# Two-layer encoder on one core: queries and keys of the first head group by seven half-sized products before the attention, kept in DRAM, with changes of order beside it

## The chip, the core and the metric

The program runs on one core of a Trainium2 chip. A core has engines that run side by side, each with its own instruction queue worked off in order: TensorE (PE, matrix products, with PEld for the loading of weights), VectorE (DVE), ScalarE (ACT), GpSimd (POOL) and SyncE (SP). SP only starts transfers here; POOL computes a little and starts the transfers that add to what is already in their destination. They meet at semaphores. The metric is the device time of one execution in microseconds (us), as a median of several executions. Before the change it is 1441.67 us (three executions, 1441.1 to 1444.09).

## What is computed

The input is x, 512 tokens by 1024 features in float32. Two layers follow each other, each with a token mixer and an MLP, and in front of each of these an RMS norm with a gain. The first mixer is the one that the change is about:

```python
def dilated_mixer(h, w_qkv, q_gain, k_gain, w_o):
    qkv = (h @ w_qkv).reshape(B, S, 3, N_GROUPS, A_HEADS, A_HEAD_DIM)   # 512 x 1024 by 1024 x 9216
    for g, (window, dil) in enumerate(DIL_CONFIGS):                     # 3 groups
        q = rope(rms_norm(qkv[:, :, 0, g], q_gain[g]), S)
        k = rope(rms_norm(qkv[:, :, 1, g], k_gain[g]), S)
        v = qkv[:, :, 2, g]
        o, lse = dilated_group(q, k, v, window, dil)                    # softmax over a dilated band
    wts = jax.nn.softmax(jnp.stack(lses, 0), axis=0)
    o = sum over g of wts[g] * o[g]
    return o.reshape(B, S, A_WIDTH) @ w_o
```

There are eight heads of 128 features in each of three groups. Per group the queries of all heads are 1024 columns of the product, the keys 1024 and the values 1024. The second mixer (multi-head latent attention) and the two MLPs (1024 to 4096, squared ReLU, back to 1024) are untouched but for one step of order.

## The kernel before

**Precision.** Products are made in three passes: each operand is split into a rounded high part and the rest (`whi`, `wlo` of a weight, made by one ACT copy and one DVE subtraction), and high by high, high by low and low by high are added up in a PSUM bank. A pass over 128 rows of the contraction and 512 columns is one matmul instruction.

**Stages.** (1) `v_phase` (line 306) norms x, turns it into `hT` and computes the values of the three groups. (2) The attention (lines 542 to 749) goes through four pairs of heads, `b` = 0 to 3. (3) The output projection, (4) the first MLP, (5) the latent attention, (6) its projection and the second MLP.

**Half-sized products in `v_phase`.** The values of a group are one product of 512 tokens by 1024 by 768 columns (the seventh and eighth head are done elsewhere). Tokens, contraction and columns are each halved, and the four quarter results are put together from seven products of quarters where plain blocks would need eight (Winograd's form of Strassen's scheme). The sums of the left operand are prepared once (`Ssp`, from `dif` and `h32`). The weight quarters `b21`, `b11`, `b12`, `b22` are loaded by SP; their sums `bT` are made by DVE (`sum1`, line 446) and by two transfers of POOL that add a further quarter into `bT` (`add_block`, line 329). `piece` (line 450) does products 5, 3, 6, 7 and 4 and puts the results together in `vo`; finished parts go to DRAM (`vall`). A product is 24 matmuls of 384 columns, and each weight quarter lies in one of five places of the ring `wq`. `dif` and `rot` (rotary tables and gains of the first group, which `tables(0, ...)` multiplies) have places of their own.

**Attention.** For each pair of heads and each group `project_in` (line 709) computes queries and keys together, 512 columns, by `qk_proj` (line 297): four token tiles of 24 matmuls, in one of four PSUM banks `acc` each; the weights come as `raw` (three places) and are split by lines 156 and 157. `qk_evac` (line 265) then works off a tile `acc`: four ACT squares with sums, three DVE products with the rotary tables (lines 276 and 279), the power -0.5 on POOL (`rstd_of`, line 131), a DVE sum and a DVE scaling (284 and 285), four PE transposes, and an ACT copy into `qkT`, which has two places. `scores` does the banded softmax; `finish` merges the groups and multiplies with the values. The loop of lines 722 to 734 projects one group ahead: the scores of group g, then the projection of g + 1, and after the third group the projection of the next pair's first group, ahead of `finish`.

**What sets the order.** The kernel is traced in this program order, and the framework's scheduler (`schedule_with_timeline_sim=True`) then orders each engine's queue by program order and by its own simulated times. So an engine's queue need not be in program order: matmuls of a later projection can stand between those of `scores`. Once built, each queue is fixed.

**End of the first MLP.** `wino` (line 759) is the MLP's own form of seven products. `fetch(..., add=True)` (line 779) has POOL start transfers that add a weight quarter in place. The tables `cgB` and `sgB` of the latent attention (lines 963 to 968) are nine POOL instructions further down in the program.

## Time and profile before

| quantity | value |
|---|---|
| median of three executions | 1441.67 us (1441.1 to 1444.09) |
| the profiled execution's own time | 1438.6 us |
| its span, from the first to the last instruction | 1436.8 us |
| mean granted TensorE clock | 0.997 |
| HBM read, written | 180.85 MB, 7.86 MB |
| `v_phase` | about 0 to 128 us of the span |
| attention, to its last merged heads | about 128 to 500 us |
| output projection and first MLP | about 500 to 894 us |
| latent attention | about 894 to 1080 us |
| its projection and second MLP | about 1080 to 1437 us |

The profile is of one execution; its own time is 3.1 us under the median. A row of the windows view gives, for a stretch of time, its length, then for PE, PEld, DVE, ACT and POOL the busy time with the count of instructions in brackets, then the granted TensorE clock, the busy share of the 16 DMA engines, and GB/s. A matmul's duration overlaps with that of the next one, so a row that shows PE fully busy can hide gaps shorter than that overlap; what a matmul costs in a dense row is the stretch divided by the count. A row of the chain of waits or of the timeline gives start, length, engine, what it is and how many instructions were merged; in square brackets stands how long the engine sat idle before it, and what ended that.

### The profile page before, as it was taken

To read this page: it belongs to the slowest core of one execution; us is meant where nothing else is said; L and a number is where in the kernel's file an instruction comes from. 1 tells how busy PE (TensorE), PEld (TensorE's weight loads), DVE (VectorE), ACT (ScalarE), POOL (GpSimd) and SP (SyncE) were. 2 spreads that over 40 slices of the span, in tenths; PEclk is the share of its full clock that TensorE was granted. 3 is DMA by queue.
4 is the path that set the end of the run, shared out by engine and by line. 5 is a ranking of instruction groups with operands and counts; after the bars stand their busy time and mean duration, and the time that the engine had idled before them with its cause. 6 is when DMAs were issued, how large, how long until landed. Compare 5 with 4: busy or idle time off the path is not lost.

```text
span 1436.8 us, 19234 instructions
## 1 busy us (share of the span) xinstructions
PE 1398.5 (97%) x7044; PEld 1184.7 (82%) x7044; DVE 928.6 (65%) x1485; ACT 746.6 (52%) x1626; POOL 213.0 (15%) x209
## 2 busy tenths in 40 slices
PE   6999999999999999999999998999999999999998
PEld 6899888988888988888888887776768888888886
DVE  6765878676886754465564758688755266475647
ACT  5553656464564623553545455787633453544543
POOL 0120121122111101020110231332201011020201
PEclk9999999999999999999999999999999999999999
DMA  9767322332322345667493934311014759394835
GB/s 310 189 167 207 117 88 72 107 93 83 117 75 68 114 134 191 175 137 216 116 235 101 213 93 84 96 31 30 30 45 149 203 112 239 90 230 135 190 90 117
DMA packets 127614, 189.97 MB, mean 132 GB/s; under 512 B 8608, under 2 KB 66208, under 8 KB 127520
## 3 DMA queue, kind: packets, MB, share of 16 engines
q1 hardware_dynamic: 106848, 150.47, 32.8%
q0 software_dynamic: 20672, 38.28, 16.2%
q8 instruction: 55, 0.90, 0.3%
q14 instruction: 39, 0.32, 0.1%
HBM read 180.85 MB, written 7.86 MB: 131 GB/s over the span
## 4 chain that ended last, share of the span: by engine, by line
PE 87%; DMA 4%; ACT 3%; DVE 3%; issue 1%; POOL 1%; SPq 0%; ACTq 0%; DVEq 0%; POOLq 0%
PE acc L184 51%; PE sc L850 11%; PE tp L850 8%; PE tp L123 4%; PE sc L422 2%; PE acc L1134 1%; PE acc L1110 1%; PE sc L1028 1%; DMA b<-in_a_w_qkv_dram 1%; PE sco L699 1%; PE sc L585 1%; PE sco L695 1%; PE tp L422 1%; DMA bT<-in_a_w_qkv_dram 1%; DMA raw<-in_a_w_qkv_dram 1%
## 5 line engine op out<-in xcount | busy, mean ns | idle before, releaser
L184 PE MATMUL acc<-whi,hT 128*128 128x512 f32 (+2 forms) x1216 | 383.2, 389 | 2.8 <-ACT hT L737 1.3
L184 PE MATMUL acc<-hT_f,whi 128*128 128x512 f32 (+1 forms) x1152 | 318.6, 366 | 1.7 <-DVE resid L913 1.2
L157 DVE TENSOR_TENSOR wlo<-raw,whi 128x1024 fp32r<-128x1024 f32 (+3 forms) x146 | 172.2, 1187 | 172.5 <-ACT whi L156 171.9
L184 PEld LDWEIGHTS acc<-whi,hT 128*128 128x128 f32 x1216 | 225.8, 188 | 44.0 <-ACT hT L737 1.9
L156 ACT ACTIVATE whi<-raw 128x1024 fp32r<-128x1024 f32 (+3 forms) x146 | 149.5, 1031 | 177.2 <-PE acc L184 83.8
L184 PEld LDWEIGHTS acc<-hT_f,whi 128*128 128x128 f32 x1152 | 208.2, 189 | 37.3 <-DVE resid L913 1.6
L184 PE MATMUL acc<-wlo,hT 128*128 128x512 f32 (+2 forms) x608 | 236.0, 389 | 0.7 <-DVE wlo L157 0.7
L794 DVE TENSOR_TENSOR wlo<-wqs,whi 128x1024 fp32r<-128x1024 f32 x112 | 137.4, 1226 | 112.9 <-ACT whi L793 112.7
L184 PE MATMUL acc<-hT_f,wlo 128*128 128x512 f32 (+1 forms) x576 | 204.9, 366 | 0.0
L793 ACT ACTIVATE whi<-wqs 128x1024 fp32r<-128x1024 f32 x112 | 118.8, 1060 | 165.6 <-PE acc L184 66.2
L850 PE MATMUL sc<-whi,asp 128*128 128x512 f32 x512 | 165.6, 391 | 4.9 <-ACT whi L793 4.7
L779 POOL DMA_DIRECT2D wqs<-in_ffn_w_dram x64 | 77.6, 1341 | 513.3 <-DVE wlo L794 331.2
L184 PEld LDWEIGHTS acc<-wlo,hT 128*128 128x128 f32 x608 | 114.4, 188 | 19.4 <-DVE wlo L157 1.0
L184 PEld LDWEIGHTS acc<-hT_f,wlo 128*128 128x128 f32 x576 | 108.5, 189 | 17.5
L850 PEld LDWEIGHTS sc<-whi,asp 128*128 128x128 f32 x512 | 96.2, 188 | 25.9 <-ACT whi L793 5.2
L850 PE MATMUL tp<-whi,asp 128*128 128x512 f32 x352 | 112.8, 392 | 0.9 <-DVE resid L824 0.9
L131 POOL TENSOR_TENSOR qrs<-rs_v,nhalf 128x4 f32<-128x4 f32 x48 | 61.2, 1279 | 305.7 <-DVE rs_v L128 265.6
L850 PE MATMUL sc<-wlo,asp 128*128 128x512 f32 x256 | 99.6, 389 | 0.0
L136 ACT ACTIVATE junk<-acc 128x128 f32<-128x128 f32 x192 | 52.8, 275 | 53.9 <-PE acc L184 48.0
L850 PEld LDWEIGHTS tp<-whi,asp 128*128 128x128 f32 x352 | 66.7, 190 | 15.3 <-DVE resid L824 1.3
L850 PE MATMUL tp<-wlo,asp 128*128 128x512 f32 x176 | 68.7, 392 | 0.0
L824 DVE TENSOR_TENSOR resid<-resid,sc 128x512 f32<-128x512 f32 x64 | 43.1, 681 | 26.3 <-PE sc L850 26.3
(229 smaller groups left out, 2171.5 us busy)
## 6 DMA issues: line engine op xcount, KB each, us to landing
wqs<-in_ffn_w_dram SPq DMA_DIRECT2D x80, 512.0 KB, 5.1
raw<-in_ffn_w_dram SPq DMA_DIRECT2D x64, 512.0 KB, 4.5
wqs<-in_ffn_w_dram POOLq DMA_DIRECT2D x64, 512.0 KB, 7.4
raw<-in_a_w_qkv_dram SPq DMA_DIRECT2D x96, 256.0 KB, 3.2
b<-in_a_w_qkv_dram SPq DMA_DIRECT2D x24, 384.0 KB, 6.2
vall<-vo SPq DMA_DIRECT2D x24, 192.0 KB, 3.6
bT<-in_a_w_qkv_dram POOLq DMA_DIRECT2D x12, 384.0 KB, 6.1
raw<-in_a_w_o_dram SPq DMA_DIRECT2D x8, 512.0 KB, 3.8
```

The costliest lines, as they stand in the source:

```text
L123: PE.transpose(o, i, ident)
L131: G.tensor_tensor(out, v[:, :n], nhalf[:, :n], op=ALU.pow)
L136: A.activation(junk, x, AF.Square, scale=1.0 / math.sqrt(dim), accum_out=out)
L156: A.activation(hi[:, :nk, :n], raw[:, :nk, :n], AF.Copy)
L157: V.tensor_tensor(lo[:, :nk, :n], raw[:, :nk, :n], hi[:, :nk, :n].bitcast(F32), op=ALU.subtract)
L184: PE.matmul(accs[o][:, oc], lhsT=lt, rhs=rt, start=(kt == 0 and p_i == 0 and hv == 0), stop=(kt == total - 1 and p_i == 2), skip_group_che ...
L422: PE.matmul(banks[t][:, :VH], lhsT=lt, rhs=rt[:, j], start=(first and k == 0 and i_ == 0), stop=(k == 3 and i_ == 2), skip_group_check=True)
L779: nc.gpsimd.dma_start(t, src, accum_op=ALU.add)
L793: A.activation(hi, x, AF.Copy)
L794: V.tensor_tensor(lo, x, hi.bitcast(F32), op=ALU.subtract)
L824: V.tensor_tensor(sl, sl, banks[t], op=op)
L850: PE.matmul(bk[t], lhsT=lt, rhs=rt[:, j], start=(first and k == 0 and i_ == 0), stop=(k == 3 and i_ == 2), skip_group_check=True)
```

## The change

Queries and keys of the first group (`g` = 0) leave `project_in`. They are computed in `v_phase`, between the values of the first group and those of the second, as two more units of seven products (a new class `Unit` stands for a weight matrix with its quarters): unit f takes query columns 512 f to 512 f + 511 as its left half and the key columns of the same range as its right half, so that a quarter is 512 columns wide and a product is 24 matmuls of 512 columns. The results go to two DRAM buffers `qk0`. In the attention `project_in(b, 0)` loads a tile of 128 tokens by 2 x 256 columns from there, for each of four token tiles, and gives it to `qk_evac` in the place of the PSUM bank; the rest of `qk_evac` is as before.

Beside it: the loop projects two groups ahead (the second group of a pair is projected before the scores of its first); `load_x(0)` comes ahead of the load of the gain; `rot` and the first group's gains are loaded, and its `tables` made, after the first unit, in the ring `xn`; `dif` lies in the ring `wq`; the ring `wq` and `vo` are 512 columns wide; and the nine POOL instructions of `cgB` and `sgB` are queued behind the last adding transfer of the first MLP (`tc.issue_after`, which orders them on POOL's queue alone).

```diff
+    qk0 = [ad.tile([S, D], F32, name=f"qk0{t}") for t in range(2)]
...
-        rot = vp.tile([P, D], F32, name="rot")
-        dif = vp.tile([P, 2, 2, 4, P], F32, name="dif")
...
+        class Unit:
+            def __init__(self, width, cols, out):
+                self.w, self.cols, self.out, self.parts = width, cols, out, {}
...
+            def tile(self, name, tag="wq", bufs=5):
+                return vp.tile([P, 4, 512], F32, tag=tag, name=nm(name), bufs=bufs)[:, :, :self.w]
...
+            def fetch(self):
+                self.b21, self.b11 = self.block(1, 0, "b21"), self.block(0, 0, "b11")
+                self.fetch_more()
+                self.bT = self.tile("bT")
...
+        vals = [Unit(VH, lambda n, g=g: w6[:, :, 2, g, VH * n:VH * n + VH],
+                     lambda i, n, g=g: by_tiles(vall[g], i, slice(VH * n, VH * n + VH))) for g in range(NG)]
+        qks = [Unit(512, lambda n, f=f: w6[:, :, n, 0, 512 * f:512 * f + 512],
+                    lambda i, n, f=f: by_tiles(qk0[n], i, slice(512 * f, 512 * f + 512))) for f in range(2)]
...
+        load_x(0)
         gain_b = gain_table(norm_mix[0:1, :].rearrange("o d -> (o d)"), D, "g_mix0")
-        load_x(0)
...
+        dif = vp.tile([P, 4, 512], F32, tag="wq", name="dif", bufs=5)
+        dif = dif.rearrange("p (n i) (k t) -> p n i k t", n=2, k=4)
         raw6.append(load_raw(*units6[3], 384))
-        nc.sync.dma_start(rot[:, 0:C_M1 - C_KEEP], consts[:, C_KEEP:C_M1])
-        g0 = rot[:, 768:1024].rearrange("p (t d) -> p t d", t=2)
-        load_gains(0, g0)
...
-        piece(0, ba)
+        piece(v0, ba)
+        rot = vp.tile([P, D], F32, tag="xn", name="rot", bufs=2)
+        nc.sync.dma_start(rot[:, 0:C_M1 - C_KEEP], consts[:, C_KEEP:C_M1])
+        g0 = rot[:, 768:1024].rearrange("p (t d) -> p t d", t=2)
+        load_gains(0, g0)
         tables(0, g0, rot[:, 0:256], rot[:, 256:768])
-        for g in range(1, NG):
...
+        for un in qks + vals[1:]:
+            un.fetch()
             bd, ba = new_banks("d"), new_banks("a")
+            both(un, 2, un.b21, bd, True)
+            put(un, 0, 0, "set", bd, False)
+            both(un, 1, un.b11, ba, True)
+            put(un, 0, 0, "add", ba, True)
+            for u in range(2):
+                sum1(un, u)
+            piece(un, ba)
...
             qkT = aw.tile([P, 4, S], F32, tag="qkT", name=nm("qkT"))
-            qk_proj(b, g, qkT, homes, junk)
+            if g:
+                qk_proj(b, g, qkT, homes, junk)
+                return qkT
+            for r in range(NT):
+                x = aw.tile([P, 2, 256], F32, tag="qk0", name=nm("qk0"), bufs=3)
+                for t in range(2):
+                    nc.sync.dma_start(x[:, t], qk0[t].rearrange("(m r) d -> m r d", r=NT)[:, r, 256 * b:256 * b + 256])
+                qk_evac(0, qkT, r, x.rearrange("p t c -> p (t c)"), homes, junk)()
             return qkT
...
-        qkT = project_in(0, 0)
+        qkT, nxt = project_in(0, 0), project_in(0, 1)
         for b in range(HA // 2):
...
-            for g in range(NG):
-                scores(b, g, qkT, Pt, stats)
-                if g + 1 < NG:
-                    qkT = project_in(b, g + 1)
+            scores(b, 0, qkT, Pt, stats)
+            qkT = nxt
+            scores(b, 1, qkT, Pt, stats)
+            qkT = project_in(b, 2)
+            scores(b, 2, qkT, Pt, stats)
             if b + 1 < HA // 2:
-                qkT = project_in(b + 1, 0)
+                qkT, nxt = project_in(b + 1, 0), project_in(b + 1, 1)
                 finish(b, Pt, stats, vs)
...
-                    nc.gpsimd.dma_start(t, src, accum_op=ALU.add)
+                    marks["sum"] = nc.gpsimd.dma_start(t, src, accum_op=ALU.add).ins
...
+            with tc.issue_after(marks["sum"]):
+                for t in range(2):
+                    for hf in range(2):
+                        gb = gr[:, t, hf * 32:hf * 32 + 32].unsqueeze(1).broadcast_to([P, NT, 32])
+                        G.tensor_tensor(cgB[:, :, t, hf * 32:hf * 32 + 32], cosB, gb, op=ALU.mult)
+                        G.tensor_tensor(sgB[:, :, t, hf * 32:hf * 32 + 32], sinB, gb, op=ALU.mult)
+                G.tensor_scalar(sgB[:, :, :, 32:64], sgB[:, :, :, 32:64], -1.0, None, op0=ALU.mult)
```

More of the change, by code (lines that the diff above doesn't have):

```diff
@@ L421, in product, with both @@
                 for i_, (lt, rt) in enumerate(((ah, hi), (ah, lo), (al, hi))):
-                    PE.matmul(banks[t][:, :VH], lhsT=lt, rhs=rt[:, j], start=(first and k == 0 and i_ == 0),
+                    PE.matmul(banks[t][:, :un.w], lhsT=lt, rhs=rt[:, j], start=(first and k == 0 and i_ == 0),
                               stop=(k == 3 and i_ == 2), skip_group_check=True)
-        def both(p, w, banks, first):
+        def both(un, p, w, banks, first):
             for u, t in ((0, 0), (0, 1), (1, 0), (1, 1)):
-                product(p, w, banks, first, u, t)
+                product(un, p, w, banks, first, u, t)
         def new_banks(chain):
@@ L509, in v_phase @@
             s2(i)
-        split(5, bT[0], 0)
-        split(5, bT[0], 1)
+        split(v0, 5, v0.bT, 0)
+        split(v0, 5, v0.bT, 1)
         for i in range(2):
```

140 lines of the change are left out of this document (59 added, 81 removed).

## The prediction

> **What bounds the kernel now.** I read the page's busy shares first, then the chain that ended last, then the windows view over the stages, then who PE waited for.
>
> ```profile
> PE 1398.5 (97%) x7044; PEld 1184.7 (82%) x7044; DVE 928.6 (65%) x1485; ACT 746.6 (52%) x1626; POOL 213.0 (15%) x209
> ...
> PE 87%; DMA 4%; ACT 3%; DVE 3%; issue 1%; POOL 1%; SPq 0%; ACTq 0%; DVEq 0%; POOLq 0%
> ```
> ```profile
> 63.00:95.00 32.00, 31.34 (x178) 30.36 (x177) 20.61 (x27) 16.71 (x24) 4.81 (x4) 1.00 0.76 199
> 95.00:128.00 33.00, 33.00 (x190) 32.78 (x190) 20.14 (x25) 16.09 (x24) 4.81 (x4) 1.00 0.57 133
> ...
> 130.00:480.00 350.00, 349.78 (x1922) 300.33 (x1921) 258.25 (x514) 191.69 (x670) 59.88 (x47) 1.00 0.32 99
> ```
> ```profile
> PE acc L184 <- DVE rs_v L128: 0.2, 1, 0.2
> ```
> ```profile
> 103.06 4.16 PE sc L422 x24
> ...
> 128.95 20.91 PE acc L184 x92
> ```
>
> The first fence says that 87% of the chain is matmuls. The second shows two units of `v_phase` and, below, the attention: there PE is busy for 349.78 of 350 us, DVE for 258.25 (74%), ACT for 191.69 (55%). The third is all that PE waited for in the attention: 0.2 us. So the attention is PE's, to the last matmul, and what is taken from PE there is won until DVE stands in the way. The fourth gives prices: a matmul of 512 columns costs 20.91 / 92 = 0.2273 us in a dense row, one of 384 columns 4.16 / 24 = 0.173 us.
>
> **The products.** Removed from the attention: 4 pairs x 4 token tiles x 24 = 384 matmuls, 384 x 0.2273 = 87.3 us of PE. Added to `v_phase`: 2 units x 7 products x 24 = 336, or 76.4 us. Net **-10.9 us**, if both places stay as dense as they are. The rest of the sum is whether they do.
>
> **The POOL tables at the end of the first MLP.** The second MLP runs the same last seven products without tables beside them, so it shows what their move is worth.
>
> ```profile
> 847.62 0.39 PE L850 MATMUL sc<-whi,asp 128*128 128x512 f32 x1
> ...
> 868.83 1.22 PE L850 MATMUL sc<-whi,asp 128*128 128x512 f32 x2 [4.73 <-ACT whi L793]
> ...
> 889.90 1.04 PE L123 MATMUL tp<-ck,xn 128*128 128x128 f32 x8
> ```
> ```profile
> 850.85 0.54 POOL L966 TENSOR_TENSOR cgB<-ck,gr 128x128 f32<-128x128 f32 x1 [26.59 <-DMA gr<-in_b_q_gain_dram]
> ...
> 859.36 1.71 POOL L968 TENSOR_SCALAR sgB<-sgB 128x256 f32<-128x256 f32 x1
> 861.03 2.50 POOL L779 DMA_DIRECT2D wqs<-in_ffn_w_dram  x2
> ...
> 884.49 0.57 POOL L131 TENSOR_TENSOR nrs<-rs_v,nhalf 128x1 f32<-128x1 f32 x1 [9.86 <-DVE rs_v L128]
> ```
> ```profile
> 868.70:872.10 3.40, 3.27 (x8) 2.63 (x9) 3.15 (x4) 1.35 (x3) 1.20 (x1) 0.50 0.19 34
> ```
> ```profile
> 881.61 8.45 PE sc L850 x36
> ...
> 1421.89 11.18 PE sc L850 x48
> ```
> ```profile
> 1393.25 0.39 PE L850 MATMUL sc<-whi,asp 128*128 128x512 f32 x1
> ```
> ```profile
> 1415.36 1.20 POOL L779 DMA_DIRECT2D wqs<-in_ffn_w_dram  x1 [1.67 <-DVE wlo L794]
> ```
> ```profile
> L219 DVE SCALAR_TENSOR_TENSOR xn<-resid,nrs,g_mix x4: 1276/1280/1284, 885.3 to 900.9; 128x1024 f32<-128x1024 f32 x4
> ```
>
> The tables hold POOL from 850.85 to 861.07; the adding transfers start at 861.03 behind them, and PE stands still for 4.73 us, after which its clock is at half for 3.4 us. From the first matmul of the seven products to their last block it is 881.61 - 847.62 = 33.99 us here and 1421.89 - 1393.25 = 28.64 us in the second MLP: **-5.3 us** when the tables go. They don't vanish: the last add ends at 1415.36 + 1.20 - 545.63 (the distance of the two starts) = 870.9, the tables then need their 10.2 us, to 881.1, and the power of the next norm, at 884.49 - 5.3 = 879.2, would wait 1.9 us. The scaling that needs it ends at 885.3 + 1.3 = 886.6, and PE asks for it at 889.90: 3.3 us of cover, so I cost this at nothing. Were the cover gone, 1.9 us would come back. Range of the term -5.4 to -3.4.
>
> **The start.**
>
> ```profile
> 0.74 0.39 SPq L232 DMA_DIRECT2D g_mix<-in_norm_mix_dram  x1
> ...
> 1.18 0.90 SPq L335 DMA_DIRECT2D xts<-in_x_dram  x2
> ...
> 7.18 1.06 ACT L136 ACTIVATE xn<-xts 128x1024 f32<-128x1024 f32 x1 [4.95 <-DMA xts<-in_x_dram]
> ...
> 10.54 1.97 PE L123 MATMUL tp<-ck,xn 128*128 128x128 f32 x8 [10.54 <-DVE xn L362]
> ```
> ```profile
> 0.00:20.00 20.00, 9.46 (x46) 8.66 (x47) 10.07 (x15) 12.24 (x21) 1.85 (x7) 1.00 0.93 296
> ```
>
> PE begins at 10.54 on a chain that begins with x. x goes out 0.44 us earlier, and no longer behind 512 KB of gain, which at 296 GB/s take 1.7 us. The gain is itself needed one step later, so -0.4 to -1.7; I take **-0.8 us**, near the lower end. The 0.5 MB of `rot` and gains leave the crowded first 30 us; I count that into the next term.
>
> **The two new units.**
>
> ```profile
> 81.28 0.61 PE L422 MATMUL sc<-whi,Ssp 128*128 128x384 f32 x2 [0.47 <-ACT whi L407]
> ```
> ```profile
> wqs<-in_ffn_w_dram POOLq DMA_DIRECT2D x64, 512.0 KB, 7.4
> ...
> bT<-in_a_w_qkv_dram POOLq DMA_DIRECT2D x12, 384.0 KB, 6.1
> ```
> ```profile
> L157 DVE TENSOR_TENSOR wlo<-raw,whi 128x1024 fp32r<-128x1024 f32 x46 | 55.7, 1218 | 34.8 <-ACT whi L156 34.6
> L279 DVE TENSOR_TENSOR t<-acc,sing 128x256 f32<-128x256 f32 x95 | 35.4, 412 | 0.0
> L276 DVE TENSOR_TENSOR t<-acc,cosg 128x512 f32<-128x512 f32 x48 | 32.8, 684 | 11.2 <-PE tp L123 5.7 <-ACT junk L136 5.1 <-PE acc L184 0.2
> ```
>
> A unit of today, 63 to 95, is 178 matmuls x 0.173 = 30.8 us in 32.0: 1.2 us lost, 0.47 of it as the gap at 81.28, where product 6 waited for its split. The last unit, 95 to 128, loses nothing, as matmuls of the first projection fill it; the second group's do so afterwards. A new unit has 38.2 us of PE (168 x 0.2273). Its DVE has 14 splits and 4 sums at 1.218 and 6 results at 0.684: 26.0 us, 68%, as in the rows above (20.61 of 32). Product 6 waits for an adding transfer behind product 5, and that takes 7.4 us for 512 KB (6.1 for 384 KB), covered by the longer products. POOL starts 8 more of them. Worse than today is the ring `wq`: `dif` takes one of five places, so that one quarter less is fetched ahead. Bounds: 2 x 1.2 = 2.4 us, and 8.4 MB a unit (four quarters of 1.05 MB, two added, two such written) at the 199 GB/s of the first row, 42.2 us for 38.2, plus about one late quarter: 12 us. I take **+5 us**, nearer to today's row. The loads of `rot` and gains and `tables(0, ...)` only move behind the first unit on SP and DVE: three loads and four DVE products of 512 columns (0.684 us) as before, needed in the attention alone, cost nothing: they lie beside the units' products, and on a DVE that is 68% busy their 2.7 us have room.
>
> **The attention with less PE.** PE's 350 us become 262.5. DVE loses 16 splits, 16 x 1.218 = 19.5 us, and keeps the rest: 238.8 us, or **91% of the new PE time** where it had 74%. ACT goes to 175 us. The 32 short loads of `qk0` take the place of 32 of `raw` on SP, and their writer is done two units earlier. Program order gives PE 21.8 us of the second group's projection while the first tile is worked off, so the start is covered. Two waits are new. With two groups ahead, the ACT copies into `qkT` of the next pair's second group wait for the place that `scores` of this pair's third group reads; behind them on ACT stand the next splits and exponentials, for which PE and DVE wait. And a load of `qk0` waits on SP for one of three places that `qk_evac` frees; behind it stand the `raw` loads. Both are covered as long as DVE keeps up, so their price is in the next term. Does DVE now hold up PE?
>
> ```profile
> 400.00:440.00 40.00, 40.00 (x217) 33.94 (x216) 33.79 (x71) 25.24 (x89) 9.62 (x7) 1.00 0.29 86
> ```
> ```profile
> 980.00:1000.00 20.00, 17.80 (x93) 13.49 (x92) 16.24 (x48) 16.06 (x55) 7.24 (x10) 1.00 0.18 54
> ```
>
> Bounds: in 40 us of this very stage DVE worked 84% and PE lost nothing (0); in the latent attention, which has little to fill with, DVE reached 81% and PE had gaps. At 81% the 238.8 us last 295, 32 us more than PE's. The stage keeps its four `acc` banks of 21.8 us of filler, and the first group's tiles no longer wait for PE, so it is nearer to the first row; I take **+6.5 us** (0 to 32).
>
> ```profile
> 184.83 2.59 POOL L131 TENSOR_TENSOR qrs<-rs_v,nhalf 128x4 f32<-128x4 f32 x1 [2.72 <-DVE rs_v L128]
> ...
> 209.34 1.01 POOL L131 TENSOR_TENSOR qrs<-rs_v,nhalf 128x4 f32<-128x4 f32 x1 [4.04 <-DVE rs_v L128]
> ```
>
> The power on POOL takes 1.01 us at its fastest here and 2.59 at other times. [...]
>
> **Sum.** -10.9 - 5.3 - 0.8 + 5 + 6.5 = **-5.5 us**. Against the profiled execution's own 1438.6 us (1.8 us outside its span) that is 1433.1; that execution lies 3.1 us under the median, so against the median of 1441.67 it is **1436.2 us**. A measurement of this kernel can tell about 0.2%, 2.9 us, from no change.
>
> **The rivals.**
> *All of it* (0.17): DVE keeps up as from 400 to 440, and the units lose what they lose today: -10.9 - 5.3 - 0.8 + 2.4 = -14.6, 1427 us. For it: 0.2 us of waits in 350. Against it: 91% is more than any 40 us here show.
> *DVE takes the attention* (0.23), the slower side: its place is 205 to 480 us, its price the time beyond 262.5. It decides from the share of time that DVE can be kept busy: the other terms give -12, so at 238.8 / 274.5 = 87% all is given back, and below it is slower. At 84% (row 400 to 440) it is 284 us, +22 - 12 = +10, 1451 us; at 81% +20, 1462 us.
> *Transfers take the units* (0.13): the units run at 199 GB/s and a quarter comes late, +12 for +5: +1.5, 1443 us, no change to be told.
> *The order does nothing* (0.05): the tables displace the norm's power instead, or the scheduler puts it behind them; -5.5 + 5.3, 1441.5 us.
>
> **How the numbers follow.** The forecast has 0.42, with a range of its own of 1431 to 1440. Faster by over 0.2%: most of forecast (0.36), all of the first rival, little of the third (0.02): 0.55. Slower: nearly all of the second (0.21) and some of the third (0.04): 0.25. Between: 0.20. The range for 8 in 10 goes from 1427 to 1455 us: it leaves out the best few cases and the second rival at and below 83%.
>
> **What would show it.** Between 840 and 900 us, shifted: no PE gap before product 6, the adds start some 5 us sooner, and no half clock. `v_phase` ends 77 to 88 us later than 128. In the attention, now about 265 to 280 us, DVE's share above 85%; PE waits on DVE (`t`, `P`, `pT`) would be the second rival, waits on `bT` or `b` in the units the third. I am wrong if the order that the scheduler built lets PE's filler run out, which no view of before can show.

## The result and the profile after: 1489.21 us, slower by 3.2%

| | before | after |
|---|---|---|
| median | 1442.88 us (1441.1 to 1444.09) | **1489.21 us** (1487.23 to 1491.03) |
| ratio, 95% interval | | **1.0321** [1.0303, 1.0339] |
| profiled execution, span | 1438.6, 1436.8 us | 1491.03, 1489.3 us |
| matmul records of PE | 7044 | 6996 |
| lost PE time, 0 to 205 us | 10.8 us | 22.2 us |
| lost PE time, 205 to 545 us | 5.3 us | **51.8 us** |
| lost PE time, rest | 42.5 us | 49.3 us |

The median before is of four executions here, one more than when the forecast was made. The forecast was 1436.2 us in a range of 1427 to 1455. **Lost PE time** is a count of mine used throughout: for each matmul of the trace, the distance from its start to the next one's start, less the distance in a dense row of its shape (0.227 us for 512 columns, 0.1735 for 384, 0.110 for 128, and likewise for the few other shapes), added up. Both gaps and slow clock fall into it. All in all it grew from 58.7 to 123.2 us, by 64.5; with the 10.9 us of matmuls that are gone that makes 53.6, and the span grew by 52.5. The rest of the difference, 1.1 us, is about the 1.25 us by which the first matmul came sooner. So the matmuls went as planned, and the time was lost between those that are left, most of it in the attention.

The fixed bounds of 205 and 545 us cut the stages of the two kernels at different places. Counted by stage, from the last product of `v_phase` to the last product with the values, the attention lost 4.5 us before and **57.9** after (its end, with a stop and a slow clock at 562 to 569 us, lies behind 545); `v_phase` 9.7 and 22.2; all that follows 44.2 and 43.0. The columns "lost" below keep the fixed bounds.

The page of the kernel after, busy shares and chain:

```profile
PE 1409.6 (95%) x6996; PEld 1191.4 (80%) x6996; DVE 958.2 (64%) x1517; ACT 769.0 (52%) x1654; POOL 220.4 (15%) x217
...
PE 76%; DVE 9%; DMA 6%; ACT 6%; issue 2%; SPq 1%; POOL 0%; DVEq 0%; ACTq 0%
```

PE's share of the chain falls from 87 to 76%. Windows of the kernel after: the end of the second new unit with the beginning of the second group's values, the values of the second and third group, the end of `v_phase` with the start of the attention, and one pair of heads, from the second merge to the third. Behind it the stretch between the same two merges of the kernel before.

```profile
128.00:166.00 38.00, 37.22 (x176) 31.79 (x175) 22.50 (x26) 18.09 (x23) 4.81 (x4) 1.00 0.73 191
166.00:205.00 39.00, 38.80 (x223) 38.22 (x222) 22.52 (x29) 19.08 (x29) 7.22 (x6) 1.00 0.65 140
205.00:245.00 40.00, 33.25 (x165) 28.92 (x163) 27.04 (x47) 21.18 (x65) 8.02 (x6) 0.96 0.79 238
...
380.56:465.09 84.53, 73.14 (x412) 63.07 (x412) 61.61 (x132) 46.08 (x172) 15.44 (x12) 0.90 0.28 83
```
```profile
319.14:409.38 90.24, 90.24 (x509) 77.95 (x508) 66.99 (x138) 50.22 (x174) 15.60 (x12) 1.00 0.31 94
```

This is the result in two rows: 96 matmuls of 512 columns fewer, 21.8 us of PE, and the pair is only 5.7 us shorter; the lost PE time in it went from 0.7 to 16.7 us. DVE works for 67.0 us of the pair before and 61.6 after, 74% and 73%. Over the pair it isn't full, and yet PE stands. Who PE waits for in the attention, the three largest:

```profile
PE tp L124 <- DVE t L287: 12.0, 5, 7.3
PE tp L124 <- DVE me L663: 10.6, 2, 5.5
PE scm L654 <- DVE P L604: 5.9, 2, 2.9
```

The timeline of the kernel after, first PE, then DVE, shows one such place (in brackets the idle time before and its releaser):

```profile
375.67 1.95 PE L599 MATMUL sc<-qkT 128*128 128x128 f32 x16
380.56 1.05 PE L654 MATMUL scm<-ca,xsel 128*128 128x4 f32 x8 [2.95 <-DVE P L604]
382.43 1.11 PE L124 MATMUL tp<-ck,t 128*128 128x128 f32 x4 [0.82 <-DVE t L287]
385.03 1.11 PE L124 MATMUL tp<-ck,t 128*128 128x128 f32 x4 [1.49 <-DVE t L287]
391.69 1.94 PE L124 MATMUL tp<-ck,t 128*128 128x128 f32 x8 [5.55 <-DVE me L663]
394.22 0.80 PE L185 MATMUL acc<-whi,hT 128*128 128x512 f32 x1 [0.59 <-DVE t L281]
```
```profile
382.29 0.76 DVE L281 TENSOR_TENSOR t<-qk,sing 128x256 f32<-128x256 f32 x2
...
385.71 0.69 DVE L278 TENSOR_TENSOR t<-qk,cosg 128x512 f32<-128x512 f32 x1
...
387.22 0.17 DVE L129 TENSOR_SCALAR rs_v<-qss 128x4 f32<-128x4 f32 x1 [0.68 <-ACT junk L137]
388.82 0.17 DVE L129 TENSOR_SCALAR rs_v<-qss 128x4 f32<-128x4 f32 x1 [1.43 <-ACT junk L137]
...
392.81 0.69 DVE L278 TENSOR_TENSOR t<-acc,cosg 128x512 f32<-128x512 f32 x1 [0.57 <-PE tp L124]
```

From 378 to 394 us PE has no matmul of a projection to do: the next one, at 394.22, waits for DVE to have read an `acc` bank (`t<-acc` at 392.81). Before that come the tiles loaded from `qk0` (`t<-qk`), which bring PE nothing but four transposes each. The mean over the pair hides what happens in this stop: there DVE is busy for 13.32 of 16 us and ACT for 15.01 (first row below). Then the clock adds to it. The other rows are windows just before and in the slow stretch, here and in `v_phase`:

```profile
378.20:394.20 16.00, 5.22 (x24) 3.96 (x24) 13.32 (x35) 15.01 (x76) 5.39 (x4) 0.61 0.37 117
378.20:381.60 3.40, 1.04 (x8) 0.97 (x8) 3.40 (x5) 2.79 (x15) 0.00 (x0) 1.00 0.82 257
381.60:398.70 17.10, 8.66 (x28) 6.51 (x28) 14.35 (x44) 14.15 (x63) 6.40 (x5) 0.50 0.19 58
...
47.10:50.50 3.40, 1.38 (x8) 1.06 (x7) 1.62 (x3) 0.00 (x0) 0.13 (x1) 1.00 1.09 213
50.50:57.30 6.80, 5.19 (x16) 5.19 (x17) 4.17 (x5) 3.26 (x6) 1.94 (x2) 0.50 0.82 145
```

The end of the first MLP is as predicted. PE's waits there, kernel before and kernel after, and POOL after: the last adding transfer now stands ahead of the tables.

```profile
PE sc L850 <- ACT whi L793: 4.7, 1, 4.7
```
```profile
PE tp L872 <- DVE resid L846: 0.9, 1, 0.9
PE sc L872 <- DVE resid L846: 0.7, 1, 0.7
```
```profile
923.40 1.20 POOL L801 DMA_DIRECT2D wqs<-in_ffn_w_dram  x1 [1.66 <-DVE wlo L816]
924.15 1.20 POOL L990 TENSOR_TENSOR cgB<-ck,gr 128x128 f32<-128x128 f32 x1
```

### The profile page after: what moved, and what is told of

Its sections match the earlier page's. It is cut to its first block, busy times and chain, and to the rows that moved or that the text cites. A ratio compares the mean times of both kernels' runs of the same rounds, so it can differ in the third digit from the quotient of the medians.

```text
span 1489.3 us, 19300 instructions
## 1 busy us (share of the span) xinstructions
PE 1409.6 (95%) x6996; PEld 1191.4 (80%) x6996; DVE 958.2 (64%) x1517; ACT 769.0 (52%) x1654; POOL 220.4 (15%) x217
## 4 chain that ended last, share of the span: by engine, by line
PE 76%; DVE 9%; DMA 6%; ACT 6%; issue 2%; SPq 1%; POOL 0%; DVEq 0%; ACTq 0%
PE acc L185 41%; PE sc L872 11%; PE tp L872 7%; PE tp L124 3%; PE sc L441 3%; DMA bT<-in_a_w_qkv_dram 2%; PE tp L441 2%; PE acc L1158 1%; PE sc L1052 1%; PE acc L1134 1%; DVE wlo L816 1%; DMA b<-in_a_w_qkv_dram 1%; PE sco L709 1%; DVE wlo L430 1%; PE acc L441 1%
## 5 line engine op out<-in xcount | busy, mean ns | idle before, releaser
L185 PE MATMUL acc<-whi,hT 128*128 128x512 f32 (+2 forms) x960 | 304.6, 392 | 5.2 <-DVE t L281 1.9
L158 DVE TENSOR_TENSOR wlo<-raw,whi 128x1024 fp32r<-128x1024 f32 (+3 forms) x130 | 153.1, 1184 | 153.4 <-ACT whi L157 152.8
L157 ACT ACTIVATE whi<-raw 128x1024 fp32r<-128x1024 f32 (+3 forms) x130 | 133.0, 1029 | 154.9 <-PE acc L185 71.9
L185 PEld LDWEIGHTS acc<-whi,hT 128*128 128x128 f32 x960 | 180.5, 191 | 38.7 <-DVE t L281 2.9
L185 PE MATMUL acc<-wlo,hT 128*128 128x512 f32 (+2 forms) x480 | 186.6, 390 | 0.0
L185 PEld LDWEIGHTS acc<-wlo,hT 128*128 128x128 f32 x480 | 91.8, 191 | 15.0 <-issue 0.2
L872 PEld LDWEIGHTS tp<-whi,asp 128*128 128x128 f32 x352 | 66.1, 188 | 16.4 <-DVE resid L846 2.7
L430 DVE TENSOR_TENSOR wlo<-b,whi 128x768 fp32r<-128x768 f32 (+1 forms) x40 | 42.3, 1063 | 35.0 <-ACT whi L429 34.8
L429 ACT ACTIVATE whi<-b 128x768 fp32r<-128x768 f32 (+1 forms) x40 | 37.2, 931 | 45.9 <-PE sc L441 18.9
```

The source lines that it names most:

```text
L157: A.activation(hi[:, :nk, :n], raw[:, :nk, :n], AF.Copy)
L158: V.tensor_tensor(lo[:, :nk, :n], raw[:, :nk, :n], hi[:, :nk, :n].bitcast(F32), op=ALU.subtract)
L185: PE.matmul(accs[o][:, oc], lhsT=lt, rhs=rt, start=(kt == 0 and p_i == 0 and hv == 0), stop=(kt == total - 1 and p_i == 2), skip_group_che ...
L429: A.activation(hi, x, AF.Copy)
L430: V.tensor_tensor(lo, x, hi.bitcast(F32), op=ALU.subtract)
L872: PE.matmul(bk[t], lhsT=lt, rhs=rt[:, j], start=(first and k == 0 and i_ == 0), stop=(k == 3 and i_ == 2), skip_group_check=True)
```

## The experiments

Eighteen variants were run. "Lost" is lost PE time in the profiled execution, 0 to 205 us and 205 to 545 us. Ratios are to the kernel before on the same chip.

| run | median us | ratio, 95% | lost 0-205 | lost 205-545 |
|---|---|---|---|---|
| after | 1489.21 | 1.0321 [1.0303, 1.0339] | 22.2 | 51.8 |
| e3_tables | 1437.92 | 0.9974 [0.9963, 0.9985] | 16.4 | 5.3 |
| e4_units_beside | 1520.67 | 1.0548 [1.0532, 1.0564] | 17.0 | 3.5 |
| e1_even | 1486.54 | 1.0311 [1.0297, 1.0324] | 18.7 | 50.4 |
| e7_swap | 1488.17 | 1.0309 [1.0278, 1.0340] | 18.1 | 53.2 |
| e2_one_ahead | 1462.84 | 1.0146 [1.0126, 1.0166] | 18.8 | 35.9 |
| e8_start | 1464.77 | 1.0147 [1.0117, 1.0178] | 18.5 | 35.2 |
| e9_weave | 1465.74 | 1.0155 [1.0119, 1.0192] | 20.7 | 35.7 |
| e10_less_dve | 1460.19 | 1.0109 [1.0093, 1.0126] | 19.1 | 36.7 |
| e11_less_act | 1468.32 | 1.0169 [1.0154, 1.0184] | 19.1 | 40.4 |
| e12_shift | 1465.54 | 1.0147 [1.0132, 1.0162] | 21.0 | 34.3 |
| e15_load2 | 1466.78 | 1.0159 [1.0123, 1.0195] | 18.1 | 34.7 |
| e13_home3 | 1449.75 | 1.0040 [1.0027, 1.0052] | 18.2 | 20.4 |
| e14_after_home3 | 1468.94 | 1.0179 [1.0146, 1.0213] | 18.5 | 38.8 |
| e17_one_home3 | 1443.72 | 0.9997 [0.9979, 1.0015] | 21.6 | 17.3 |
| e18_inplace | 1453.97 | 1.0071 [1.0048, 1.0094] | 18.3 | 25.0 |
| e16_one_home4 | 1446.94 | 1.0024 [1.0011, 1.0038] | 18.5 | 20.4 |
| e19_one_inplace3 | 1476.69 | 1.0227 [1.0192, 1.0263] | 16.8 | 45.8 |
| e20_home4_start4 | 1441.03 | 0.9991 [0.9982, 1.0000] | 17.4 | 17.9 |

The kernel before has 10.8 and 5.3. That e3_tables, whose program is that of before in these 205 us, has 16.4 there shows how far a single execution may differ: 4.7 of it lie at 140 to 160 us. Nor is the profiled execution always near the median: that of e3 is the second slowest of its twelve (1441.69 us), that of e10 the slowest of its four (1464.79), that of e13 the fastest of its ten (1446.06).

### The parts alone: tables, and units without their use

e3_tables is the kernel before with the tables queued behind the adding transfers:

```diff
+            with tc.issue_after(marks["sum"]):
...
```

> The kernel before with one edit, the nine POOL instructions of the tables cgB and sgB queued behind the last adding transfer of the first MLP. As predicted: the 4.73 us gap of PE and the half clock behind it go, 5.3 us less than the kernel before, ratio 0.9963. Rival: the tables delay the power of the next norm instead, and nothing is won, ratio 1.000.

Measured: 0.9974 of 1441.86 us, 3.7 us faster (interval 2.2 to 5.3). The term holds, near its lower end.

e4_units_beside has the changed kernel's `v_phase`, units and tables, but the attention of before, which computes the first group once more and never reads `qk0` (with the loop of e2_one_ahead below).

```diff
-            if g:
-                qk_proj(b, g, qkT, homes, junk)
-                return qkT
-            for r in range(NT):
...
+            qk_proj(b, g, qkT, homes, junk)
```

> The v_phase of the changed kernel, with its two new units and its order, and the tables behind the adds, but the attention of the kernel before: the first group's queries and keys are computed a second time in the attention, and the results of the units are written to DRAM and not read. It prices the units. As predicted (5 us of stalls): 1442.9 + 76.4 + 5 - 5.3 - 0.8 = 1518 us. If the units lose what the changed kernel's trace suggests (12 us more than the kernel before up to 205 us): 1525 us. If the loss in the changed kernel's attention comes from the order of queues behind the units rather than from the missing products, this one shows gaps of PE between 205 and 560 us as well, and lies above 1540 us.

Measured 1520.67. Against 1441.86: +78.8, of which 76.4 are the units' matmuls; with the 3.7 of the tables and about 1 of the start given back, the stalls of the units are some **7 us**, give or take 3 by the intervals of e3 and e4. The attention of this kernel from 205 to 520 us:

```profile
205.00:520.00 315.00, 314.66 (x1699) 268.99 (x1699) 231.72 (x459) 173.60 (x590) 55.53 (x43) 1.00 0.33 104
```

So the units are not where the time went. Without the first group's matmuls, and with this attention's density, the kernel would take 1520.67 - 87.3 = 1433.4 us; the changed one takes 56 us more.

### The order

e1_even spreads the projections between the scores; e7_swap projects the second group of the next pair before its first; e2_one_ahead goes back to the loop of before, one group ahead.

```diff
@@ e1_even
...
             scores(b, 0, qkT, Pt, stats)
-            qkT = nxt
-            scores(b, 1, qkT, Pt, stats)
-            qkT = project_in(b, 2)
-            scores(b, 2, qkT, Pt, stats)
+            last = project_in(b, 2)
+            scores(b, 1, nxt, Pt, stats)
...
+                qkT = project_in(b + 1, 0)
+            scores(b, 2, last, Pt, stats)
...
+                nxt = project_in(b + 1, 1)
...
@@ e7_swap
-                qkT, nxt = project_in(b + 1, 0), project_in(b + 1, 1)
+                nxt, qkT = project_in(b + 1, 1), project_in(b + 1, 0)
@@ e2_one_ahead
-        qkT, nxt = project_in(0, 0), project_in(0, 1)
+        qkT = project_in(0, 0)
...
-            scores(b, 0, qkT, Pt, stats)
-            qkT = nxt
-            scores(b, 1, qkT, Pt, stats)
-            qkT = project_in(b, 2)
-            scores(b, 2, qkT, Pt, stats)
+            for g in range(NG):
+                scores(b, g, qkT, Pt, stats)
+                if g + 1 < NG:
+                    qkT = project_in(b, g + 1)
             if b + 1 < HA // 2:
-                qkT, nxt = project_in(b + 1, 0), project_in(b + 1, 1)
+                qkT = project_in(b + 1, 0)
```

> The changed kernel with another order of the same work in the attention's loop: the third group's projection right behind the scores of the first group, the next pair's first group (loads and tile work) behind the scores of the second, the next pair's second group behind the scores of the third, then finish. Theory A (bunching): the changed kernel puts the tile work of two groups, eight tiles, between the scores of the third group and finish, all four acc banks stand full and PE has nothing left to do; spread evenly, the PE gaps around 377 to 394 us and 462 to 478 us go, and with them the half clock behind them: 30 to 45 us less than the changed kernel, 1445 to 1460 us. Theory B (total load): DVE needs 91% of PE's time whatever the order, so it stays within 10 us of the changed kernel's 1489 us.

> The changed kernel with one line swapped: after the scores of a pair's third group the next pair's second group is projected first and its first group's loaded tiles come behind it. Theory B (banks): in the changed kernel PE stops because the first group's four tiles, which bring no matmuls, stand on DVE and ACT ahead of the four tiles that free the acc banks. Then the banks come free some 15 us sooner, the stops near 381 to 392 and 465 to 476 us shrink to under half, and the time is 1462 to 1476 us. Theory W (work): DVE and ACT have too much to do in the attention whatever the order, and it stays at 1484 to 1494 us. Both could fail: if the scores of the next pair's first group then come late and PE waits for them instead, it is no better, with the waits on qkT.

> The changed kernel with the loop order of the kernel before (one group ahead: scores, projection of the next group; the next pair's first group ahead of finish), so that finish has no products of a projection beside it. Theory A (bunching): the tile work is spread again, four tiles between two scores, but PE has only transposes while finish runs, about 10 to 20 us a pair three times; 1460 to 1490 us. Theory B (total load): within 10 us of 1489 us.

e1 and e7 changed next to nothing (1.0311 and 1.0309): my theory that the loaded tiles only stood ahead of the wrong tiles fell. One group ahead is 26 us better (two executions of e2), a pair of it takes 76.81 us where it took 84.53 (first row). The second row is one of e2's two longest stops, the third a stretch of the kernel before:

```profile
375.14:451.95 76.81, 71.44 (x414) 61.96 (x413) 61.99 (x131) 45.58 (x171) 17.77 (x12) 0.96 0.30 92
375.80:387.80 12.00, 6.63 (x22) 4.95 (x22) 11.95 (x31) 8.82 (x30) 2.33 (x2) 0.72 0.39 120
```
```profile
376.80:392.80 16.00, 16.00 (x85) 13.60 (x84) 16.00 (x31) 11.52 (x42) 2.01 (x2) 1.00 0.43 131
```

In e2's stop DVE is full, 11.95 of 12 us. But in the kernel before it is full for 16 us on end, and PE loses 0.1 us there, as it has matmuls of a projection to do. So a full DVE alone does not stop PE; in e2's stop this filler had run out as well.

e8_start moves the first pair's loads of values behind its projections; e9_weave keeps one group ahead and puts each loaded tile of the next pair behind one projected tile of this pair's third group.

```diff
@@ e8_start
-            vs = v_load(b)
+            vs = v_load(b) if b else None
...
+            vs = vs or v_load(b)
@@ e9_weave
...
+            def evac(r, acc):
+                qk_evac(g, qkT, r, acc, homes, junk)()
+                if beside is not None:
+                    tile0(b + 1, r, beside)
...
```

> The variant with one group ahead (1462.84 us), with the loads of the first pair's values moved behind the projection of its third group in program order. Theory S (start): PE loses about 13 us between 227 and 250 us because the loads of the first group's tiles and of the second group's weights stand on SP behind 2 MB of values. Then PE's excess there falls from 13.6 to under 5 us and the time is 1450 to 1456 us. If it is the chain of the first tiles themselves (loads, ACT, DVE, PE, with nothing else for PE), the time stays at 1459 to 1464 us.

> The variant with one group ahead, with the four loaded tiles of the next pair's first group woven one by one between the tiles of this pair's third group, so that each stretch of 24 matmuls stands beside one loaded tile; the same work in all. Theory B (banks, order): the stops at 376 to 384 and 452 to 461 us, and most of those behind the scores, go; the stop at the start stays (nothing is changed there): 1440 to 1450 us. Theory W (work): DVE is busy for 80% of the attention in either order, and it stays at 1458 to 1466 us.

Neither gained anything: 1464.77 and 1465.74 us. In e8 the weights did go out sooner, and the start (205 to 255 us) lost 11.2 us, where e2 lost 13.6. In e9 the long stops became many short ones, without a slow clock in the middle pairs, and a pair still took 75.36 us. So neither bunching alone nor the clock is the cause.

### DVE's work or the wait for a place

Windows of e9_weave between two merges, and what DVE waited for from 250 to 520 us:

```profile
389.72:465.08 75.36, 71.01 (x414) 60.29 (x413) 62.02 (x132) 45.63 (x169) 19.20 (x12) 1.00 0.27 85
```
```profile
DVE t L278 <- PE tp L124: 16.5, 9, 2.5
```

DVE is busy for 82% of the pair, near the 81% at which my second rival gives 1462 us, and idles longest before the first product of a tile, for PE's transposes. Those free the place of `t1`, in which a tile is rotated: there are two. Four variants of e9 tell work from places. e10 leaves out the sine half of the first group's rotation with its sum, 6 us of DVE a pair; e11 leaves out three of four squares of the first group's tiles, 6 us of ACT a pair. e12 moves 4 us from DVE to ACT, e13 gives `t1` a third place.

```diff
@@ e10_less_dve
-        for hf in range(2):
+        for hf in range(2 if g else 0):
...
-            V.tensor_tensor(t1, t1, t2, op=ALU.add)
+            if g:
+                V.tensor_tensor(t1, t1, t2, op=ALU.add)
...
@@ e11_less_act
-        for c in range(4):
+        for c in range(4 if g else 1):
...
@@ e12_shift
-                V.tensor_copy(pT, tp)
+                A.activation(pT, tp, AF.Copy)
...
-            V.tensor_copy(oT[:, 2 * b + h], o)
+            A.activation(oT[:, 2 * b + h], o, AF.Copy)
@@ e13_home3
...
-            return [aw.tile([P, 4, DH], F32, tag=t, name=nm(t)) for t in ("t1", "t2")]
+            return [aw.tile([P, 4, DH], F32, tag=t, name=nm(t), bufs=n) for t, n in (("t1", 3), ("t2", 2))]
...
-                x = aw.tile([P, 2, 256], F32, tag="qk0", name=nm("qk0"), bufs=3)
+                x = aw.tile([P, 2, 256], F32, tag="qk0", name=nm("qk0"), bufs=2)
```

> The woven variant (1465.74 us; per pair 75.4 us with PE idle for 8 to 10, DVE busy 62.0, ACT 45.6) without the sine half of the rotation and without its sum for the first group: three DVE instructions of 1.51 us less for each of 16 tiles, 6.0 us a pair, nothing else. Theory D (DVE's work): the attention lasts as long as DVE at some 82% needs, so a pair becomes about 68 us and the time 1437 to 1446 us. Theory L (the chain of a tile through ACT, POOL, DVE, PE and back): a tile's chain gets only about 0.7 us shorter, as the sums of squares run beside the rotation, and the time is 1458 to 1466 us.

> The woven variant with one sum of squares in place of four for each tile of the first group (the other three heads are scaled by the first one's): three ACT squares with their sums, 1.49 us, less for each of 16 tiles, 6.0 us of ACT a pair, DVE's work the same. Theory D: no change beyond 5 us, 1460 to 1467 us. Theory L: the chain of a tile begins with these squares and is 1.5 us shorter each time, 1440 to 1455 us.

> The woven variant with the copies of the transposed probabilities of the second and third group and of the pair's result out of PSUM made by ACT and not by DVE; nothing is left out: 4 x 0.68 + 2 x 0.69 = 4.1 us a pair from DVE to ACT, which then has some 49 of 75 us. Theory D: a pair gets some 4 to 5 us shorter, 1445 to 1453 us. Theory L, or a bound that lies on ACT: 1461 to 1472 us.

> The woven variant with three places in place of two for the tile that PE transposes (t1), paid for with one place less for the loaded tiles. DVE idles 5.8 us a pair for the transposes that free such a place. Theory D: the place is the link by which PE holds up a DVE that has no time to spare, so the 5.8 us go and a pair is up to 6 us shorter, 1443 to 1458 us. If DVE then only waits at the next link: 1461 to 1467 us.

With three DVE instructions fewer in each of 16 tiles, 24 us of DVE in all, e10 is 5.5 us faster, between the two bands. Its trace, of an execution 4.6 us above its median, doesn't show this gain: a pair takes as long there as in e9, with DVE 4.7 us less busy. So DVE's work counts for far less than its length in this order. e11 and e12 gain nothing. e13 gains **16 us**. Windows of e10, then of e13 with its DVE wait:

```profile
386.83:463.21 76.38, 72.33 (x413) 62.10 (x412) 57.30 (x120) 45.81 (x169) 16.54 (x12) 0.98 0.27 83
```
```profile
379.87:450.87 71.00, 69.53 (x413) 60.35 (x412) 61.80 (x132) 46.45 (x169) 16.14 (x12) 1.00 0.30 92
```
```profile
DVE t L278 <- PE tp L124: 6.4, 5, 1.6
```

DVE works just as much in 71.00 us as in 75.36, at 87%, and the wait for the place fell from 16.5 to 6.4 us. What decided here was not how much DVE has to do. These four were run in e9's order alone: whether less work for DVE or ACT would shorten the long stops of the changed kernel or of e2, in which one of the two is full, was not tried.

Is it the place, and does it hold in the other orders? e15_load2 has the last line of the diff above alone; e14_after_home3 and e17_one_home3 are the changed kernel and e2 with all of e13's lines; e18_inplace rotates a loaded tile in its load place, so that it needs none of `t1`:

```diff
@@ e18_inplace
...
-            return [aw.tile([P, 4, DH], F32, tag=t, name=nm(t)) for t in ("t1", "t2")]
+            t2 = aw.tile([P, 4, DH], F32, tag="t2", name=nm("t2"))
+            return (aw.tile([P, 4, DH], F32, tag="t1", name=nm("t1")) if x is None else x.rearrange("p t (h d) -> p (t h) d", h=2)), t2
...
```

> The woven variant (1465.74 us) with two places for the loaded tiles in place of three and t1 as it was: the control for the run with three t1 places. Theory P: nothing gained, 1463 to 1470 us. If fewer loads ahead were what helped: 1446 to 1455 us.

> The changed kernel in its own order (1489.21 us) with three places for t1, the tile that PE transposes, and two for the loaded tiles. Theory P (places): the loaded tiles take places of t1 that only PE's transposes free, DVE stops for them, and the acc banks stay full. Then the place helps in every order, by 16 us or more as here four loaded tiles come in a row: 1460 to 1473 us. Theory O (order): with two groups ahead eight tiles come in a row whatever the places, and the place brings under 8 us: 1481 to 1490 us.

> The variant with one group ahead, not woven (1462.84 us), with three places for t1 and two for the loaded tiles. Theory P: as in the woven order, 1443 to 1452 us. If only the weaving made the place worth anything: 1457 to 1464 us.

> The woven variant in which a loaded tile is rotated in its own place (the sine products first, then the cosine product over the tile itself) and takes no place of t1; two places of t1 and three load places as in the changed kernel, the same instructions, nothing left out. Theory P: the loaded tiles no longer hold places that the projected tiles need, and the time is at that of three t1 places or below, 1438 to 1451 us. Against it: the cosine product now waits for the sums of squares that read the tile, about 2 us of ACT, and a load place comes free only behind the transposes; if that weighs as much, 1455 to 1467 us.

The control gains nothing (1466.78); e13 differs from it in the places of `t1` alone and is 17 us faster. The place is worth 20 us in the changed kernel's own order (1489.21 to 1468.94) and 19 with one group ahead (1462.84 to 1443.72). The order is worth 26 us with two places and 25 with three: the two causes add. What it is in the order of two groups ahead that costs so much is open, as e1 and e7, two other forms of it, were no better. e18, with the loaded tiles out of the contended ring, gains 12, less than the place. A good part of the place's gain lies at the start: from 205 to 255 us e2 lost 13.6 us and e17 5.2, e9 11.9 and e13 4.5.

One reserve: the scheduler builds all queues anew for each variant, and with a third place PE's queue has another order too: the matmuls of e15 stand in e9's order to the last one, those of e13 in another from the first tile of the attention on. Between 205 and 545 us DVE's wait for the place fell by 10.1 us from e9 to e13 and by 5.5 from e2 to e17 (10.5 to 5.0), while the lost PE time fell by 15.3 and 18.6; at the start (205 to 255 us), where 7.4 and 8.4 us of that gain lie, no trace of the four has this wait. The runs show that the place brings the gain, not how much of it is the wait itself and how much the order that it allows.

### What is left

e16_one_home4 (four places of `t1`, one load place), e19_one_inplace3 (e18's rotation, three places, one group ahead) and e20_home4_start4, which is e16 with the first pair's tiles in the places of `pT`:

```diff
@@ e20_home4_start4
-                x = aw.tile([P, 2, 256], F32, tag="qk0", name=nm("qk0"), bufs=1)
+                x = aw.tile([P, 512], F32, tag="qk0" if b else "pT", name=nm("qk0"), bufs=1 if b else 4)
```

> One group ahead with four places for t1 and one for the loaded tiles (1443.72 us with three and two). Theory P (places still bind): another 3 to 6 us, 1437 to 1441 us. If DVE's work binds from three places on: 1442 to 1446 us. If a single load place makes the tiles wait for their loads (2 to 3 us of landing for each of 16, half of it hidden): 1450 to 1465 us.

> One group ahead with three places for t1, and the loaded tiles rotated in their own two places, so that they take none of the three; nothing left out. Theory P: 1437 to 1442 us. If DVE's work binds from three places on, or the waits of the cosine product for the squares weigh as much: 1443 to 1452 us.

> One group ahead, four places for t1, one load place for the later pairs, and for the first pair's four tiles the four places of pT, which nothing uses until the first product with the values. If the single load place holds the start: its 11.6 us of lost PE time (220 to 260 us) fall to 5 or less, and the time goes from 1446.94 to 1438 to 1442 us, below the kernel before. If the start is held by the chain of its first tiles through ACT, DVE and POOL: 1444 to 1448 us.

e16 isn't faster than e17, but its loss lies elsewhere: 11.6 us at the start (205 to 255 us) where e17 lost 5.2, and 5.4 in the three pairs behind (255 to 500) where e17 lost 8.7. e19 is 33 us slower than e17, with stops of up to 8.2 us back; PE waited there for the first group's tiles and the exponentials. I have no tested reason for it, and it speaks against a theory in which places of `t1` are all that counts. e20 came into its band at 1441.03 us, but the start still lost 9.7 us, where I expected 5 or less: the single load place is at most a small part of it, and the band was met in part by luck, as only 1.9 of the 5.2 us by which the two profiled executions differ in lost PE time lie at the start. Windows of e20, start and a middle pair:

```profile
205.00:255.00 50.00, 44.09 (x208) 36.79 (x207) 38.17 (x71) 25.59 (x81) 10.11 (x8) 0.93 0.63 196
367.78:437.35 69.57, 68.53 (x415) 60.13 (x413) 61.70 (x132) 44.97 (x172) 17.11 (x12) 1.00 0.34 105
```

No version with the half-sized queries and keys beat the kernel before by more than a measurement tells. e3_tables, the tables alone, is at 0.9974, with its whole interval below 1. As e20 has the moved tables too, the products gained nothing in it.

## Why the prediction was wrong

**Products, -10.9: right.** 48 matmuls fewer, 7044 to 6996.

**Tables, -5.3: right in mechanism, -3.7 measured** (2.2 to 5.3), in the range of -5.4 to -3.4. The wait for the split is gone, and no norm waits in its place. In the profiled execution of the kernel after, all that follows the attention lost only 1.2 us less than before, as another slow stretch, at 1153.0 us, came instead; e3's twelve executions are the better measure.

**Start, -0.8: right in direction.** PE's first transposes come at 9.29 us, 1.25 us sooner. In the other builds with this start they come at 8.17 to 9.34 us, up to 2.4 us sooner, which is more than the term's range; no run has this step alone, so its price in the end is not shown.

```profile
9.29 1.97 PE L124 MATMUL tp<-ck,xn 128*128 128x128 f32 x8 [9.29 <-DVE xn L384]
```

**New units, +5: about right**, 7 us by e4 in bounds of 2.4 to 12, but partly by luck. The matmuls of the new units lost 7.2 us in the kernel after and 4.3 in e4; the largest stall is not there but in the first group's unit of values, whose adding transfer now lands late: 3.64 us where the kernel before lost 1.48, with 6.8 us at half clock from 50.5 us on. That `dif` in the ring did it is not shown, as it was not tried alone. The rival "Transfers take the units" showed its sign, waits on `bT`, but PE's two waits through them came to 5.6 us in all.

```profile
52.11 1.01 PE L441 MATMUL sc<-whi,Ssp 128*128 128x384 f32 x2 [3.64 <-ACT whi L429]
```

**Attention with less PE, +6.5 (0 to 32): the step that failed.** It measured 57.9 - 4.5 = +53.4 us of lost PE time over the stage (46.5 within 205 to 545 us). Rows of its start, kernel after, timeline of PE and of ACT:

```profile
245.53 1.94 PE L124 MATMUL tp<-ck,t 128*128 128x128 f32 x8 [7.28 <-DVE t L287]
249.73 0.58 PE L588 MATMUL sc<-qkT 128*128 128x128 f32 x1 [2.26 <-ACT qkT L296]
```
```profile
232.16 0.31 ACT L137 ACTIVATE junk<-qk 128x128 f32<-128x128 f32 x1 [6.46 <-DMA qk<-qk]
```

Four sentences of this step fell:

- "The stage keeps its four `acc` banks of 21.8 us of filler, and the first group's tiles no longer wait for PE, so it is nearer to the first row; I take **+6.5 us** (0 to 32)." This is what sized the term, and both halves failed. PE ran out of filler: from 375.8 to 394.2 us it had no matmul of a projection. And the first group's tiles go on waiting for PE: a tile holds a place of `t1` until PE has transposed it. A third place is worth 20 us in this kernel's order (e14), one group ahead 26 (e2), and the two together bring it back to the time of the kernel before (e17).
- "Program order gives PE 21.8 us of the second group's projection while the first tile is worked off, so the start is covered." The start lost 13.4 us (205 to 255 us). Four loaded tiles, not one, come before the first scores, ACT stood 6.46 us for the load of one of them, and PE was out of work from 238.2 to 245.5 us.
- "Both are covered as long as DVE keeps up, so their price is in the next term." The order of two groups ahead cost 25 to 26 us by itself, with DVE at 73%. That it cost this through these two waits is not shown.
- "Does DVE now hold up PE?" was asked of DVE's share of the whole stage. That share was no bound: 73% in the changed kernel, 82% in e9, 87% in e13 and 89% (61.70 of 69.57) in e20, for the same work. In the stops shown above DVE or ACT is nearly full and PE has nothing else to do; the mean over the stage hides that. I listed two new waits, for `qkT` and for `qk0`, and not the old one whose cover I removed. It stood in a row that I showed: DVE's first product of a tile waited 5.7 us for PE's transposes (`<-PE tp L123 5.7`), while PE, with matmuls of its own in its queue, lost 0.2 us.

**The rival "DVE takes the attention"** had the right sign and stage, and its price at 81%, 1462 us, is near that of e2 and e9; that is luck. As a bound by DVE's share over the stage it is refuted: 24 us less of DVE's work (e10) brought 5.5, and one more place 16 with the same work. That DVE, or ACT, holds up PE within a stop, when the filler has run out, is what the rows of the stops show. The clause at the end of the prediction, that PE's filler runs out in the order built, is what happened; it had no price there.

**The powers on POOL**, of which two rows of the prediction show one of 2.59 and one of 1.01 us, in the kernel after (fastest, median, longest in ns):

```profile
L132 POOL TENSOR_TENSOR qrs<-rs_v,nhalf x48: 997/1007/3050, 225.9 to 508.9; 128x4 f32<-128x4 f32 x48
```

The median, 1.007 us, is where the fastest is, as in the kernel before (1.008). In e9 it is 1.31 us and in e13 too; e13 is the faster by 16 us for all that.

## What to carry to other kernels

When work is taken from the bounding engine, look for what its instructions covered: list every ring whose places that engine frees, and ask of each whether the producer can still run ahead when the filler between two of its instructions is gone. In these runs one place of `t1` more took away 13 to 19 us of lost PE time (51.8 to 38.8, 35.7 to 20.4, 35.9 to 17.3). The same reserve holds: the order of the queues changed with the place. The busy share of the second engine over a stage does not answer the question: it was the same work at 73 and at 89%. Look at the shares within the stops, and at what the engine that stops has left to do there.

## What the runs showed of the hardware

The stretches in which PE's granted clock was 0.50, and which end within the trace, lasted 3.4, 6.8, 13.7 and 17.1 us in the kernel after, that is one, two, four and five steps of about 3.41 us; before had two of 3.4 us. PE was not always idle in the 3.4 us ahead of one: before the stretches at 50.5 and 381.6 us it was busy for 1.38 and 1.04 of the 3.4 us. And a step in which PE was busy for a part only did not always end a slow stretch: in the five steps of the one from 381.60 us PE was busy for 1.13, 1.11, 0.15, 2.83 and 3.41 of 3.41 us, and in the two of the one from 50.5 us for 1.81 and 3.41. In each of the eight slow stretches of the kernel after that end within it, PE was busy for 2.98 us or more of the last step.
